# TensorE's order is written out by the program from the first mixer's projection on

## The chip, the cores and the metric

The kernel runs on one core of a Trainium2 chip. The time is the device time of one execution in microseconds (us): the median of three runs. PE is TensorE's matmul side, PEld its weight loads, DVE is VectorE, ACT ScalarE, POOL GpSimd, SP the engine that issues most of the DMAs. A code such as L466 is a line of the kernel.

## What is computed

Two decoder layers over 1024 tokens of width 1024. Only the first layer's mixer is touched by the change:

```python
h = rms_norm(x, norm_mix[l]) * (1.0 + scale_m) + shift_m   # scale_m, shift_m, ...: c_act @ w_ada + b_ada
# even_mixer:
proj = h @ w_in
u, q, k, v = jnp.split(proj, ...)
y = s5_ssm(u...);  y = gelu(y);  y = y * sigmoid(y @ w_glu)
q = apply_partial_rope(rms_norm(q, q_norm), cos, sin)       # k the same
o = diff_attention(q, k, v, lam, ...)                       # 4 heads, causal, 128-query blocks
mix = jnp.concatenate([y, o], axis=-1) @ w_out
x = x + gate_m * mix
x = x + gate_f * swiglu(...)                                # the first FFN; then the second layer
```

## The kernel before

A dense product in f32 accuracy is made of three matmuls for each slice of 128 inputs: the weights and the activations are each split into a rounded part and a rest (`whi`, `wlo` and the like), and `mm3g` (L466) adds hi x hi, lo x hi and hi x lo in PSUM. The weights are split by ACT (L449) and by DVE or POOL (L450).

The kernel is a set of Python generators. `weave(main, fill, rate)` advances `fill` by `rate` steps for each step of `main`, so the text of the program already interleaves the stages. What comes of it on an engine is decided by a scheduler: it runs a model of the engines and takes, for each engine, what it holds to be ready first. From the first FFN on (`manual_schedule` for PE, L1736) this is switched off for PE alone: there its instructions stand in the order in which the program issues them. DVE, ACT, POOL and SP are ordered by the scheduler throughout. Every engine works through its own list.

The stages that lie between the start and the first FFN, in the order of the program's text (`mix0`, L1147):

- `u_proj`: eight tiles `pu` of 24 matmuls, woven with `mods_acc`, which loads columns of `w_ada` (`mwt`), multiplies and adds them up on DVE into `macc` (L334, L336) and lets PE sum over the partitions (`mpc`, L391). Two such sums of 32 small matmuls are issued here, each after eight loads of 512 KB.
- `attn_proj(0)`, woven one to one with the four quarters of the state-space part (`s5_quarter`: `pS` L808, a scan on DVE L823, products on DVE and POOL L831 to L833, `pY` L840 and L842). `attn_proj(1)` follows, woven with the attention of heads 0 and 1 for the first 512 tokens.
- the attention of heads 2 and 3, woven with the gate's product `pz` (`glu`).
- the output projection `pout` (`out_proj(0)`), woven with 14 steps of the attention of the last 512 tokens.

`attn_proj(hp)` makes 24 tiles of 128 tokens by 256 columns: eight of q, eight of k, eight of v. A tile of q or k, in the order of the text, is this (L928 to L968):

```python
pt = pa.tile(...)                    # psA: two PSUM buffers
self.mm3(pt, ..., KT)                # 24 matmuls pq
nc.scalar.activation(sq, pt, AF.Square)                 # ACT  L945  asq
v.tensor_reduce(ss, sq, ...); v.tensor_scalar(ss, ...)  # DVE  L947, L948  ass
g_.tensor_tensor(rs, ss, mhalf, op=ALU.pow)             # POOL L950  ars
v.tensor_tensor(qn, pt, rs, op=ALU.mult)                # DVE  L952  aqn
g_.tensor_tensor(ra, ...); g_.tensor_tensor(rb, ...)    # POOL L959 to L962: rotary, into aqn
for h in range(2):
    nc.tensor.transpose(tp[:, h, :], qn[...], ident)    # PE   L965  tq
nc.scalar.activation(dst, tp, AF.Copy, scale=...)       # ACT  L967
yield
```

A tile of v has the 24 matmuls and one copy. An attention step has scores (`sps`, L1001 and a mask L1006), a maximum on DVE, exponentials on ACT, a combination on DVE, then transposes `wt` (L1039), a copy on ACT, the products with the values `po` (L1044), a norm over DVE, ACT and POOL, and the transpose `ot` (L1062).

Of the kernel before, what the change touches and what calls it, by code (L numbers as in the profile page):

```python
# [146 lines left out]
class Trunk:  # L147
# [1570 lines left out]
    def run(self):  # L1718
        st = self.stages
        nc, pool = self.nc, self.nc.gpsimd  # L1720
        self.setup()
        self.start()
        ffn0, ffn1, mix1 = "ffn0" in st, "ffn1" in st, "mix1" in st
        none = iter(())
        fs = {}
# [7 lines left out]
            drain(self.mods_acc(0, (2 * D, 6 * D), self.pz, "z", self.mods_tiles("C"), nc.sync))  # L1733
        if "mix0" not in st:
            self.late_vectors()
        ms = self.tc.manual_schedule(engines={mybir.EngineType.PE})  # L1736
        ms.__enter__()

        def mods1():
            if "mix0" in st:  # L1740
                self.close(self.ap)
                self.close(self.at)
                self.close(self.pss)
            self.close(self.pz)
            self.pr = self.open("m1p", 1, PSUM)
            if "mix0" in st:
                self.inject = self.glu_units(1)
            yield from self.mods_acc(1, (0, 6 * D), self.pr, "R", self.mods_tiles("C"), pool)
# [115 lines left out]
```

## Time and profile before

| | |
|---|---|
| median of 3 runs | 3177.56 us (3169.1 to 3178.48) |
| the profiled execution | 3189.24 us, span 3187.3 us |
| PE busy | 2976.2 us, 93% |
| DVE, ACT, POOL busy | 1921.7, 1193.9, 889.5 us |
| chain that ended last | PE 72%, DVE 12%, issue 6%, DMA 5% |
| mean granted TensorE clock | 0.965 |

The last matmul of `u_proj` starts at 143.6 us, the last of `attn_proj(1)` at 408.7, the sums that begin the first FFN's norm at 532.4, the first FFN's first matmul at 546.9. A busy PE isn't a PE at its peak: at the lower of its two clocks the same matmul is busy for longer. The granted clock is 1.00 at 2.4 GHz and 0.50 at 1.2 GHz.

### The profile page before, as it was taken

How to read it: one execution, taken by the hardware profiler on the slowest of the kernel's cores; microseconds unless marked ns; L12 is line 12 of the kernel's file. 1: busy time of each engine (PE TensorE's matmuls, PEld its weight loads, DVE VectorE, ACT ScalarE, POOL GpSimd, SP SyncE). 2: the span in 40 equal slices, each digit the busy share in tenths (PEclk: the TensorE clock that was granted, in tenths of full speed). 3: DMA queues.
4: the chain of work that ended last, by engine and by line, in shares of the span. 5: the costliest groups of instructions: out<-in, count | busy, mean ns of one | idle time of the engine just before them, and what ended most of it. 6: DMA issues, size and time to landing. Idle time of an engine off the chain costs nothing.

```text
span 3187.3 us, 50746 instructions
## 1 busy us (share of the span) xinstructions
PE 2976.2 (93%) x19326; PEld 2250.0 (71%) x19326; DVE 1921.7 (60%) x3982; ACT 1193.9 (37%) x2446; POOL 889.5 (28%) x1007
## 2 busy tenths in 40 slices
PE   4879989999999998999999999989999999999999
PEld 1678866776777766677666777666776677777777
DVE  7744645555674645777777545467777874434443
ACT  3212334333223644444444345544444443322222
POOL 6562402000110302344434342024344444200000
PEclk7989978999999999999999999999999999999999
DMA  6853221223573444212222244522222213533332
GB/s 242 213 134 67 69 71 53 80 73 105 179 232 113 156 146 126 71 56 77 74 67 80 81 148 136 155 85 75 70 60 81 75 59 93 167 90 93 96 103 93
DMA packets 489857, 338.39 MB, mean 106 GB/s; under 512 B 44280, under 2 KB 451088, under 8 KB 488592
## 3 DMA queue, kind: packets, MB, share of 16 engines
q1 hardware_dynamic: 474288, 304.75, 32.2%
q0 software_dynamic: 7632, 25.68, 2.6%
q10 hardware_dynamic: 7696, 4.74, 0.6%
q8 instruction: 153, 2.51, 0.3%
q14 instruction: 88, 0.72, 0.1%
HBM read 292.63 MB, written 42.47 MB: 105 GB/s over the span
## 4 chain that ended last, share of the span: by engine, by line
PE 72%; DVE 12%; issue 6%; DMA 5%; ACT 3%; POOL 2%; SPq 0%; ACTq 0%; DVEq 0%; POOLq 0%
PE pg L466 13%; PE pu L466 13%; PE pd L466 12%; PE pkrv L466 8%; PE pout L466 5%; PE pq L466 3%; PE sps L1001 3%; DMA mwt<-in_w_ada 2%; PE po L1044 1%; ACT whi L449 1%; PE pR L1666 1%; PE pA L1592 1%; PE pR L1651 1%; PE pA L1495 1%; DVE wlo L450 1%
## 5 line engine op out<-in xcount | busy, mean ns | idle before, releaser
L449 ACT CAST whi<-wraw 128x1024 fp32r<-128x1024 f32 (+2 forms) x472 | 401.9, 852 | 887.7 <-PE pg L466 186.3
L466 PE MATMUL pd<-dd,whi 128*128 128x512 f32 x1408 | 463.3, 410 | 14.8 <-DVE x L534 10.7
L450 DVE TENSOR_TENSOR wlo<-wraw,whi 128x1024 fp32r<-128x1024 f32 (+2 forms) x288 | 296.1, 1029 | 271.9 <-ACT whi L449 255.4
L450 POOL TENSOR_TENSOR wlo<-wraw,whi 128x1024 fp32r<-128x1024 f32 (+2 forms) x184 | 326.0, 1773 | 461.5 <-ACT whi L449 420.1
L466 PE MATMUL pg<-fhi,whi 128*128 128x512 f32 x704 | 301.5, 428 | 13.0 <-DVE sg L521 10.8
L466 PEld LDWEIGHTS pd<-dd,whi 128*128 128x128 f32 x1408 | 254.0, 189 | 80.6 <-ACT whi L449 19.3
L466 PE MATMUL pu<-fhi,whi 128*128 128x512 f32 x704 | 295.4, 420 | 1.4 <-ACT ev L1365 0.8
L466 PE MATMUL pg<-fhi,wlo 128*128 128x512 f32 x704 | 283.4, 403 | 6.3 <-DVE wlo L450 6.3
L466 PE MATMUL pu<-fhi,wlo 128*128 128x512 f32 x704 | 279.1, 396 | 3.7 <-POOL wlo L450 2.2
L466 PE MATMUL pg<-flo,whi 128*128 128x512 f32 x704 | 281.7, 400 | 0.0
L466 PE MATMUL pd<-dd,wlo 128*128 128x512 f32 x704 | 279.4, 397 | 2.1 <-DVE oss L1053 0.9
L466 PE MATMUL pu<-flo,whi 128*128 128x512 f32 x704 | 277.7, 394 | 0.0
L534 DVE SCALAR_TENSOR_TENSOR x<-pd,mod,x 128x512 f32<-128x512 f32 x192 | 143.4, 747 | 122.9 <-PE pd L466 121.9
L466 PE MATMUL pkrv<-xh,whi 128*128 128x512 f32 x384 | 165.4, 431 | 12.3 <-ACT ev L1365 6.4
L466 PEld LDWEIGHTS pg<-fhi,whi 128*128 128x128 f32 x704 | 135.2, 192 | 47.2 <-DVE sg L521 12.0
L466 PEld LDWEIGHTS pg<-fhi,wlo 128*128 128x128 f32 x704 | 135.1, 192 | 40.3 <-DVE wlo L450 8.7
L466 PEld LDWEIGHTS pd<-dd,wlo 128*128 128x128 f32 x704 | 133.0, 189 | 38.8 <-DVE wlo L450 3.8
L466 PEld LDWEIGHTS pu<-fhi,whi 128*128 128x128 f32 x704 | 132.9, 189 | 36.3 <-issue 2.4
L466 PEld LDWEIGHTS pu<-fhi,wlo 128*128 128x128 f32 x704 | 132.6, 188 | 35.7 <-POOL wlo L450 3.0
L466 PE MATMUL pkrv<-xh,wlo 128*128 128x512 f32 x384 | 154.6, 403 | 1.3 <-DVE wlo L450 1.3
L466 PE MATMUL pkrv<-xl,whi 128*128 128x512 f32 x384 | 154.4, 402 | 0.0
L466 PEld LDWEIGHTS pg<-flo,whi 128*128 128x128 f32 x704 | 135.3, 192 | 25.3
(460 smaller groups left out, 6084.1 us busy)
## 6 DMA issues: line engine op xcount, KB each, us to landing
wraw<-in_ffn_w_gate SPq DMA_DIRECT2D x88, 512.0 KB, 3.7
wraw<-in_ffn_w_up SPq DMA_DIRECT2D x88, 512.0 KB, 3.8
wraw<-in_ffn_w_down SPq DMA_DIRECT2D x128, 256.0 KB, 2.7
mwt<-in_w_ada POOLq DMA_DIRECT2D x48, 512.0 KB, 5.4
mwt<-in_w_ada SPq DMA_DIRECT2D x32, 512.0 KB, 5.4
wraw<-in_ffn_w_down SPq DMA_DIRECT2D x64, 192.0 KB, 2.5
kd<-ev SPq DMA_DIRECT2D x48, 256.0 KB, 2.0
xs<-x SPq DMA_DIRECT2D x8, 1024.0 KB, 6.3
```

What stands on the lines that cost most here:

```text
L449: nc.scalar.copy(hi, raw)
L450: (eng or nc.vector).tensor_tensor(lo, raw, hi.bitcast(F32), op=ALU.subtract)
L466: nc.tensor.matmul(out, lhsT=w(k), rhs=x(k), start=first and i == 0, stop=last and i == n - 1)
L534: nc.vector.scalar_tensor_tensor(x[:, n, :], pd, gate[:, n : n + 1], x[:, n, :], op0=ALU.mult, op1=ALU.add)
L1001: nc.tensor.matmul(sp[:, c0 : c0 + n], lhsT=qT[r : r + 64, hd, o : o + P], rhs=kT[r : r + 64, hd % 2, c0 : c0 + n], start=True, stop=not l ...
L1044: nc.tensor.matmul(po, lhsT=wt[:, j - j0, :], rhs=vt[:, j, P * (hd % 2) : P * (hd % 2) + P], start=(j == 0), stop=(j == i))
L1495: nc.tensor.matmul(pas[h][:, c, :], lhsT=FS[rows[h], c, :], rhs=AR[h][rows[h], c, :], start=True, stop=True)
L1592: te.matmul(px[32 * g : 32 * g + 32], lhsT=XF[:, g, :], rhs=QE[:, g], start=True, stop=True)
L1651: te.matmul(pp[rows[h], :], lhsT=AR[h][:, c, 0:64], rhs=XH[h][:, c, :], start=True, stop=True)
L1666: te.matmul(ph[rows[h], :], lhsT=BE[:, c, rows[h]], rhs=XU[h][:, c, :], start=True, stop=True)
```

## The change

The two lines that switch the scheduler off for PE are moved from behind the first mixer to ahead of it. `start()` stays scheduled; from `mix0()` on PE's instructions stand in the order of the text. No instruction is added or removed.

```diff
@@ run @@
         self.setup()
         self.start()
+
+        ms = self.tc.manual_schedule(engines={mybir.EngineType.PE})
+        ms.__enter__()
         ffn0, ffn1, mix1 = "ffn0" in st, "ffn1" in st, "mix1" in st
...
         if "mix0" not in st:
             self.late_vectors()
-        ms = self.tc.manual_schedule(engines={mybir.EngineType.PE})
-        ms.__enter__()
-
         def mods1():
```

The first place is PE at the start of `attn_proj(0)`. `pq_` and a number is one tile's PSUM buffer, `tq` its transposes, `mpc` the second sum of `mods_acc`. Before, the first tile's last matmul, the ends of the third and fourth tile, and what follows them:

```order
L466 MATMUL pq_1521<-whi_1517,m0lo_107_537 128x256
...
L466 MATMUL pq_1651<-whi_1517,m0lo_107_537 128x256
...
L466 MATMUL pq_1705<-whi_1517,m0lo_107_537 128x256
L965 MATMUL tq_1561<-ident,aqn_1553 128x128 x2
L391 MATMUL mpc_1456<-ones,macc_1139 32x1 x32
L808 MATMUL pS_1628<-UT_1565,s5E_13_157 64x128 x8
```

And now, from the end of `u_proj` on:

```order
L466 MATMUL pu_1426<-m0hi_169_1016,wlo_1357 128x512
L391 MATMUL mpc_1458<-ones,macc_1141 32x1 x32
L250 MATMUL vp_1501<-ident,vr_1492 128x104
L466 MATMUL pq_1523<-whi_1513,m0hi_104_534 128x256
...
L466 MATMUL pq_1523<-whi_1519,m0lo_107_537 128x256
L965 MATMUL tq_1563<-ident,aqn_1555 128x128 x2
L466 MATMUL pq_1586<-whi_1513,m0hi_104_534 128x256
...
L466 MATMUL pq_1586<-whi_1519,m0lo_107_537 128x256
L965 MATMUL tq_1626<-ident,aqn_1618 128x128 x2
L808 MATMUL pS_1630<-UT_1567,s5E_13_157 64x128 x8
```

The first tile's transposes stood behind four tiles; now every tile's transposes stand right behind its own 24 matmuls and ahead of the next tile's, and the same holds for all 32 tiles of q and k. The second sum `mpc` stood behind four tiles too, and now stands ahead of the first.

The second place is PE where `attn_proj(1)` has ended and `pz` begins. Before, behind the last `pq`:

```order
L1044 MATMUL po_4374<-vt_2852,wts_4377 128x128
L1001 MATMUL sps_4515<-kT_2851,qT_1505 128x512
...
L1001 MATMUL sps_4530<-kT_2851,qT_1505 128x512
...
L466 MATMUL pz_4348<-gluh_4328,whi_4344 128x512
L466 MATMUL pz_4348<-gluh_4329,whi_4344 128x512
L466 MATMUL pz_4348<-gluh_4328,wlo_4345 128x512
L466 MATMUL pz_4348<-gluh_4328,whi_4344 128x512
```

And now:

```order
L1001 MATMUL sps_4318<-kT_2853,qT_1507 128x128
...
L466 MATMUL pz_4350<-gluh_4330,whi_4346 128x512
L466 MATMUL pz_4350<-gluh_4331,whi_4346 128x512
L466 MATMUL pz_4350<-gluh_4330,wlo_4347 128x512
L1001 MATMUL sps_4354<-kT_2853,qT_1507 128x128
...
L1039 MATMUL wt_4377<-ident,pe_2844 128x128
L1001 MATMUL sps_4381<-kT_2853,qT_1507 128x256
```

Before, head 2 was done by then (the scores are those of its last block) and `pz` stood in two runs of 24 matmuls; now head 2 only begins here (a score over 128 keys is its first block), and `pz` is dealt out in threes and sixes over the steps of heads 2 and 3. Behind it `pout` follows in one run in the text's order, where before 36 of its matmuls stood between the steps of head 3. From the first FFN on PE's order is the same in both.

## Rows read from the trace of the kernel before

**Rows 1.** Busy time by stretch; columns: stretch, length, engines, granted clock, DMA, GB/s.

```profile
144.00:179.00 35.00, 19.34 (x165) 18.39 (x165) 17.99 (x22) 3.30 (x7) 29.41 (x29) 0.75 0.84 224
179.00:305.00 126.00, 114.51 (x846) 100.77 (x847) 57.07 (x126) 28.04 (x56) 46.49 (x81) 0.92 0.43 84
305.00:409.00 104.00, 100.69 (x860) 89.20 (x858) 63.03 (x190) 42.80 (x120) 42.15 (x88) 0.98 0.25 72
409.00:533.00 124.00, 115.56 (x460) 76.89 (x459) 60.59 (x137) 45.67 (x107) 19.37 (x17) 0.81 0.23 69
```

**Rows 2.** Instruction groups, 144 to 410 us: busy us, mean ns, idle before, releaser.

```profile
L466 PE MATMUL pq<-whi,m0hi 128*128 128x256 f32 x384 | 116.7, 305 | 16.4 <-DVE aqn L952 16.4
L842 PE MATMUL pY<-H,s5D 64*128 64x128 f32 x128 | 22.0, 316 | 5.6 <-DVE H L833 5.6
L1001 PE MATMUL sps<-kT,qT 64*128 64x128 f32 (+3 forms) x46 | 18.2, 475 | 0.0
L840 PE MATMUL pY<-UT 128*128 128x128 f32 x64 | 14.3, 313 | 0.0
...
L965 PE MATMUL tq<-ident,aqn 128*128 128x128 f32 x64 | 12.3, 279 | 0.0
...
L808 PE MATMUL pS<-UT,s5E 128*64 128x128 f32 x128 | 10.7, 299 | 0.0
L823 DVE TENSOR_TENSOR_SCAN s5tm<-rho,s5tm 128x128 f32<-128x128 f32 x32 | 10.6, 400 | 0.0
...
L1044 PE MATMUL po<-vt,wts 128*128 128x128 f32 x42 | 6.5, 279 | 0.0
...
L1039 PE MATMUL wt<-ident,pe 128*128 128x128 f32 x21 | 3.9, 272 | 0.0
```

**Rows 3.** Timeline, two tiles' norm and rotary: start us, duration us, engine, line, operation.

```profile
189.14 0.28 PE L466 MATMUL pq<-whi,m0lo 128*128 128x256 f32 x1
189.47 0.38 ACT L945 ACTIVATE asq<-pq 128x256 f32<-128x256 f32 x1
...
193.16 0.32 POOL L962 TENSOR_TENSOR aqn<-ara,arb 128x64 f32<-128x64 f32 x1
...
206.71 0.38 ACT L945 ACTIVATE asq<-pq 128x256 f32<-128x256 f32 x1 [9.18 <-PE pq L466]
...
211.03 0.32 POOL L962 TENSOR_TENSOR aqn<-ara,arb 128x64 f32<-128x64 f32 x1
```

**Rows 4.** Timeline of PE within one tile, behind a wait.

```profile
201.84 0.55 PE L466 MATMUL pq<-whi,m0hi 128*128 128x256 f32 x1 [5.37 <-DVE aqn L952]
202.19 0.41 PE L466 MATMUL pq<-wlo,m0hi 128*128 128x256 f32 x1
202.40 0.41 PE L466 MATMUL pq<-whi,m0lo 128*128 128x256 f32 x1
...
205.81 0.28 PE L466 MATMUL pq<-whi,m0hi 128*128 128x256 f32 x1
205.93 0.28 PE L466 MATMUL pq<-wlo,m0hi 128*128 128x256 f32 x1
```

**Rows 5.** Timeline of DVE: the second eight loads of `w_ada`, first, fourth, fifth, last.

```profile
145.09 1.14 DVE L334 TENSOR_SCALAR macc<-mwt,cact 128x1024 f32<-128x1024 f32 x1 [2.00 <-DMA mwt<-in_w_ada]
...
157.64 1.28 DVE L336 SCALAR_TENSOR_TENSOR macc<-mwt,cact,macc 128x1024 f32<-128x1024 f32 x1 [2.42 <-DMA mwt<-in_w_ada]
...
166.50 2.88 DVE L336 SCALAR_TENSOR_TENSOR macc<-mwt,cact,macc 128x1024 f32<-128x1024 f32 x1
...
176.79 1.28 DVE L336 SCALAR_TENSOR_TENSOR macc<-mwt,cact,macc 128x1024 f32<-128x1024 f32 x1 [2.15 <-DMA mwt<-in_w_ada]
```

**Rows 6.** The late attention steps: a 10 us stretch, then two transposes that begin a step.

```profile
450.00:460.00 10.00, 9.37 (x21) 4.82 (x21) 4.24 (x14) 3.48 (x13) 0.55 (x1) 0.50 0.00 1
...
449.44 0.42 PE L1039 MATMUL wt<-ident,pe 128*128 128x128 f32 x1
457.92 0.63 PE L1039 MATMUL wt<-ident,pe 128*128 128x128 f32 x2
```

## The prediction

> **What bounds the kernel now.** I read the page's busy shares first, then the chain that ended last, then busy time by stretch, then the groups and the timeline of the stretch that the change reaches. PE is busy for 93% of the span and holds 72% of the chain, so what PE loses ahead of the first FFN is paid at the end: from there on its order is the same in both, and nothing later has slack that would take a delay up. The stretch to read is 144 to 533 us, from the first `pq` to the first FFN's norm. Here PE is busy for 19.3 of 35, 114.5 of 126, 100.7 of 104 and 115.6 of 124 us [rows 1]: ragged at the start, then nearly closed, with 0.75, 0.92, 0.98 and 0.81 as the granted clock.
>
> It is closed because the scheduler puts matmuls behind something else whenever an operand isn't ready. The 64 transposes `tq` never once keep PE idle (their idle time is 0.0), while `pq` waits 16.4 us for a PSUM buffer to be read out by `aqn` [rows 2]. That zero is what the change touches: the order shows up to four tiles of `pq` between a tile and its `tq` before, and none now.
>
> **Step 1, the transposes of q and k.** What lies between a tile's last matmul and its `tq` is a chain over ACT, DVE, POOL, DVE and POOL. In a quiet place the last matmul begins at 189.14 and ends at 189.42, the square begins at 189.47, and the last rotary instruction ends at 193.16 + 0.32 = 193.48 [rows 3]: 4.06 us, and with a hand-off of 0.1 us (estimated from the gap of 0.05 at the chain's other end) 4.15 us. In a busier place the square begins at 206.71 and the chain ends at 211.35 [rows 3]: 4.64, with both ends 4.8 us. PE's list is worked off in order, so it stands for all of this, 32 times, with the next tile's 24 matmuls behind. I take 4.8, since DVE serves the state-space scan, the weight splits and the attention too; the bounds are 4.15 and 6.1, the latter with half of one quarter's scan (10.6 us / 8 = 1.3) [rows 2] in front.
>
> The Trainium skill says (TensorE: Matmul & The Clock Gate, "Step-by-step: what each phase is for") that only weight loads are pulled ahead and matmuls stay in program order. No run here shows a matmul that was free to pass a waiting one. By that rule the wait counts in full; without it, step 1 would be near zero and the kernel near 3178 us, which is the last rival below.
>
> **Step 2, the clock of the bursts between these waits.** After an idle time of 5.37 us a tile's matmuls follow each other at 0.21 us (202.19 to 202.40), and only from 205.81 at 0.12 [rows 4]: the lower clock for some 3.8 us, then the higher one. Before the stall the clock had not been low for good: the whole stretch averages 0.92 [rows 1]. A tile costs 24 x 0.117 = 2.8 us at the higher clock and 24 x 0.213 = 5.1 at the lower one. With a wait of nearly 5 us ahead of each, I take 3.8 us at the lower clock (18 matmuls) and the other 6 at the higher (0.7): 4.5 us. With 0.3 for the two transposes a tile of q or k takes 4.5 + 4.8 + 0.3 = 9.6 us, and 32 of them 307. Bounds: 2.8 + 4.15 + 0.3 = 7.25, so 232; 5.1 + 6.1 + 0.4 = 11.6, so 371.
>
> A rule of the skill bears on that (same page, "HAM oscillation — how this bites in real kernels"): bursts shorter than the waits between them start at half rate every time. By it the 32 bursts lose 32 x (4.5 - 2.8) = 54 us, and without it nothing; the rows above agree for one burst.
>
> **Step 3, the second `mpc`.** It needs eight loads of `w_ada`, added up on DVE at 145.09, ..., 157.64, 166.50, ..., 176.79 [rows 5]. Before, four tiles ran meanwhile; now the first `pq` is behind it. The fifth add was late (8.9 us after the fourth) since DVE was busy with the tiles' own work, which now comes later; the other six intervals average (31.7 - 8.9) / 6 = 3.8 us. So the sum is ready at about 145.1 + 7 x 3.8 + 1.3 = 173 us, and PE is idle from 144: 29 us. Bounds: 25 (intervals of 3.2) and 34 (as before, 178).
>
> **Step 4, what else stands in the stretch of 265 us, from 144 to 409 [rows 1].** The 16 tiles of v have no `tq` and run on: 16 x 2.8 + 3 for two slow starts = 48 (45 to 60). The state-space matmuls are 22.0 + 14.3 + 10.7 = 47 busy us [rows 2], some of it overlap of pipelined matmuls: 43 (35 to 60). They come behind a `tq`, not ahead of it, so they hide no wait. Attention now has 8 steps here where 11 ran; 11 took 18.2 + 6.5 + 3.9 = 28.6 us [rows 2], so 8 take 21 (16 to 32). Each quarter's scan, 10.6 / 4 = 2.7 us on DVE [rows 2], is queued ahead of one tile's chain: 12 (0 to 25). Sum: 29 + 307 + 48 + 43 + 21 + 12 = 460 us, against 265: +195. The ends all low: 353, or +88; all high: 582, or +317.
>
> **Step 5, heads 2 and 3, `pz` and `pout`.** Before, the scheduler had spent `pz` and a good part of `pout` early, so the last steps stood bare: at clock 0.50, one every 8.5 us [rows 6]. Now heads 2 and 3 (8 steps and the run-out) stand here with `pz` among them, and block 1's first steps fall among dense `pout`. 8 steps at about 8 us (less than 8.5, being shorter), 6 for the run-out, 192 `pout` of 512 columns at twice 0.117 = 45, and 12 for the other attention work: 127 against 124 [rows 1]. I take +3 (-15, if the filler keeps the clock up, to +20).
>
> Nothing else moves: the DMAs keep their order but for a few, and from the FFN on all is only later. So +198 on the profiled execution's 3189.24 us, or 3387; that execution stands 11.7 us above the median shown, so I forecast 3177.6 + 198 = 3376 us.
>
> **The rivals.**
> - The clock holds and the chains stay quiet: tiles at 7.25 us, the other terms low or as taken: 232 + 27 + 46 + 38 + 18 + 4 = 365, +100, 3278 us. For it: in 305 to 409 the clock was 0.98 [rows 1]; against it, that PE had no gaps there.
> - The chains are crowded: PE now waits for DVE, ACT and POOL, and in the second half attention's exponentials, maxima and copies queue among the chains (DVE 63.0, ACT 42.8 of 104 us [rows 1]). At 11.6 us a tile: 371 + 32 + 55 + 50 + 26 + 20 = 554, +289, 3467 us. Against it: none of these engines is over 61% busy.
> - Faster: the bare stretch of step 5 goes. From 440 to 488 us PE runs at half clock on attention alone; if `pz` and `pout`, now dealt out, keep it at the higher one, about half of it comes back, 25 us: 3153 us. It decides only if a tile's wait costs under 25 / 32 = 0.8 us; the shortest chain in the rows is 4.06.
> - It does nothing: PE passes the waiting transposes, or waits where it waited anyway. 3178 us. Against it: the order, and that PE already idles on `aqn` with other work in its list.
>
> **How the numbers follow.** The forecast 0.77, the holding clock 0.10, the crowded chains 0.10, faster 0.02, nothing 0.01. The forecast's own range is 3300 to 3440; taking in the first two rivals to their middle, 3280 to 3460. Faster than before by over 0.3% (what a measurement of this kernel can tell from none) 0.02, within it 0.01, slower 0.97.
>
> **What would show it.** Right: PE idle of 4 to 6 us ahead of `tq`, 32 times, put down to POOL's L962, some 150 us in sum; a granted clock well under 0.9 from 173 to the last `pq`; one wait near 29 us ahead of the second `mpc`; the last `pq` near 604 us; from the first FFN on the same lengths as before. Wrong: idle ahead of `tq` near 0, or of 3 us and less; a first `pq` ahead of 165 us; or a clock near 1.00 with tiles at 7 us.

## The result and the profile after

The kernel with TensorE's order given by the program from the projection on takes 3450.9 us (median of 4; 3445.1 to 3455.1) against 3174.1 for the kernel before (median of 4; 3169.1 to 3178.5): 1.0858 times as long, 95% interval 1.0830 to 1.0885, or 277 us more. The forecast was 3376 us, with 3300 to 3440 as its own range and 3280 to 3460 with its first two rivals taken in. The profiled execution took 3451.7 us (span 3449.9, mean clock 0.928), 262.5 more than that of before.

The time is lost ahead of the first FFN, as forecast. These are the busy times by stretch of the changed kernel, columns as in [rows 1]; up to 656 us stands what stood up to 409 before, then heads 2 and 3 and the output projection:

```profile
144.00:177.40 33.40, 10.53 (x153) 8.40 (x153) 23.42 (x12) 1.53 (x2) 18.72 (x9) 0.60 0.98 280
177.40:435.20 257.80, 178.64 (x930) 158.86 (x930) 59.12 (x127) 27.68 (x54) 48.82 (x91) 0.68 0.20 38
435.20:656.00 220.80, 145.85 (x853) 122.42 (x853) 64.83 (x176) 45.69 (x117) 39.20 (x88) 0.72 0.12 34
...
656.00:790.00 134.00, 114.99 (x478) 76.67 (x477) 67.36 (x161) 50.85 (x120) 16.91 (x17) 0.85 0.21 64
```

The first three are 512 us where [rows 1] shows 265, the last 134 where 124 stood. PE was idle for 30.5 of the 265 (265 less 234.5 busy) and is idle for 177 of the 512, and it is busy for 100.5 us more on nearly the same work, at a granted clock of 0.60 to 0.72 where it had 0.75 to 0.98. So there are two losses, idle time and a low clock.

From the FFN on hardly anything differs. This is the group of its first matmuls (count, ns min/median/max, first and last start), in the kernel before and in the changed one:

```profile
L466 PE MATMUL pg<-fhi,whi x704: 387/393/797, 547.0 to 3146.3; 128*128 128x512 f32 x176
```

```profile
L466 PE MATMUL pg<-fhi,whi x704: 387/394/797, 804.0 to 3408.2; 128*128 128x512 f32 x176
```

The first start is 257.0 us later, the last 261.9. The 5 us between have no place that I found. The kernels below, with the same order there, spread over 2632 to 2646 us from that first start to the end, so up to 14 us of a difference between two traces can lie there and not in what was changed.

The groups of 140 to 660 us that answer to [rows 2] (busy, mean ns, idle before):

```profile
L466 PE MATMUL pq<-whi,m0hi 128*128 128x256 f32 x384 | 138.7, 361 | 0.0
...
L842 PE MATMUL pY<-H,s5D 64*128 64x128 f32 x128 | 38.2, 448 | 1.2 <-DVE H L833 1.2
L1001 PE MATMUL sps<-kT,qT 64*128 64x128 f32 (+3 forms) x37 | 24.1, 749 | 0.0
...
L965 PE MATMUL tq<-ident,aqn 128*128 128x128 f32 x64 | 20.5, 420 | 148.9 <-POOL aqn L962 148.9
```

The zero ahead of `tq` has become 148.9 us, and the matmuls of every group shown are longer: `pY` 448 ns for 316, `sps` 749 for 475.

One tile of q shows both losses. The timeline of the changed kernel, answering to [rows 3] and [rows 4]:

```profile
456.83 0.42 PE L466 MATMUL pq<-wlo,m0hi 128*128 128x256 f32 x1
457.05 0.41 PE L466 MATMUL pq<-whi,m0lo 128*128 128x256 f32 x1
...
460.21 0.28 PE L466 MATMUL pq<-whi,m0lo 128*128 128x256 f32 x1
460.33 0.28 PE L466 MATMUL pq<-whi,m0hi 128*128 128x256 f32 x1
...
460.91 0.28 PE L466 MATMUL pq<-whi,m0lo 128*128 128x256 f32 x1
461.29 0.38 ACT L945 ACTIVATE asq<-pq 128x256 f32<-128x256 f32 x1 [3.27 <-PE pq L466]
...
464.79 0.32 POOL L962 TENSOR_TENSOR aqn<-ara,arb 128x64 f32<-128x64 f32 x1
465.16 0.69 PE L965 MATMUL tq<-ident,aqn 128*128 128x128 f32 x2 [3.96 <-POOL aqn L962]
```

The tile starts at the lower level, one matmul each 0.21 us, and only its last matmuls follow each other at 0.12. Then PE stands for 3.96 us, until the tile's own chain from the square to the last rotary instruction is done, and the clock is low again afterwards.

### The profile page after: what moved, and what is told of

It is laid out like the page before. It is cut to its first block, busy times and chain, and to the rows that moved or that the text cites. A ratio compares the mean times of both kernels' runs of the same rounds, so it can differ in the third digit from the quotient of the medians.

```text
span 3449.9 us, 50768 instructions
## 1 busy us (share of the span) xinstructions
PE 3069.2 (89%) x19326; PEld 2326.5 (67%) x19326; DVE 1942.1 (56%) x3982; ACT 1200.4 (35%) x2446; POOL 883.8 (26%) x1007
## 4 chain that ended last, share of the span: by engine, by line
PE 73%; DVE 13%; DMA 4%; ACT 4%; issue 3%; POOL 3%; SPq 0%; ACTq 0%; DVEq 0%; POOLq 0%
PE pg L466 13%; PE pu L466 13%; PE pd L466 11%; PE pkrv L466 7%; PE pq L466 5%; PE pout L466 4%; PE sps L1001 2%; DMA mwt<-in_w_ada 2%; ACT whi L449 1%; DVE wlo L450 1%; PE pY L842 1%; PE po L1044 1%; POOL ars L950 1%; PE pR L1666 1%; DVE macc L336 1%
```

## The experiments

Three theories were set against each other. Theory 1: the 32 waits of `tq` and the low clock around them are the loss. Theory 2: any order given by the program makes PE wait here, on one chain or another. Theory 3: the clock would be low in any case. Times are medians; each has the kernel before run beside it on the same chip (3171 to 3176 us).

### The transposes one tile later

```
@@ attn_proj
-                tp = self.ps.tile([P, 2, P], F32, tag="mm", name=self.nm("tq"))
...
+                late.append((qn, dst, n))
@@ behind the next tile's mm3
+                if len(late) >= 1:
+                    turn(*late.pop(0))   # the two transposes and the copy
```

> The changed kernel, with one thing moved in the program's text: the two transposes (tq) of a q or k tile, and the copy behind them, stand after the matmuls of the next tile instead of straight behind their own tile's norm and rotary chain. Theory 1 (the loss is the 32 waits of tq behind their own chain, 148.9 us in the changed kernel's trace, and the low clock that comes with these gaps, some 99.5 us more PE busy time in the stretch up to the last pq): nearly all of both comes back, the waits of tq fall below 30 us, the stretch runs near the 0.9 clock, and the time is 3215 to 3270 us; the wait of the second mpc (some 30 us) and some 10 us in heads 2 and 3 stay. Theory 2 (any order given by the program makes PE wait here, because the state-space and attention steps stand between the tiles with chains of their own): the waits move from tq to pY, wt and sps, over 100 us of idle stays, and the time is 3350 us or more.

3248.6 us (3245.2 to 3251.3), 1.0236 [1.0221, 1.0252] of the kernel before: 202 us of the 277 are back, as theory 1 had it. Its stretch from 144 us to the last `pq`, and the waits from 140 to 560 us, which takes in part of heads 2 and 3 (sum, times, longest):

```profile
144.00:468.00 324.00, 257.51 (x1937) 227.89 (x1938) 142.53 (x315) 73.23 (x172) 110.05 (x188) 0.83 0.32 82
```

```profile
PE mpc L391 <- DVE macc L336: 33.9, 2, 20.9
PE tq L930 <- POOL aqn L972: 27.2, 11, 6.6
PE wt L1046 <- DVE pe L1040: 12.2, 9, 3.0
```

Only the place of the 64 transposes, and of the copies behind them, differs from the changed kernel. Their wait fell from 148.9 to 27.2 us, and PE's busy time in the stretch from 335 to 257.5 us on the same matmuls: the clock came back with the gaps gone. The state-space and attention steps took little over: of the 12.2 us of `wt` only 3.9 lie in the stretch, where the changed kernel has 1.5, far from theory 2's 100.

### The gaps filled with matmuls that compute nothing

```
                 tp = self.ps.tile([P, 2, P], F32, tag="mm", name=self.nm("tq"))
+                for i in range(14):
+                    nc.tensor.matmul(tp[:, i % 2, :], lhsT=self.ident, rhs=self.ident, start=True, stop=True)
```

> The changed kernel with 14 matmuls of 128 columns that compute nothing of use (identity by identity into the tile that the transposes then overwrite) ahead of each tq, so that PE is at work for some 3.7 us (14 x 0.26) of the 3.9 us in which it now waits; the order and every wait on data stay. Theory 1: the wait as such costs 148.9 us and is now filled instead of idle, so that part stays; but PE has no gap, the clock rises to 2.4 GHz in the tiles, and the 99.5 us that the slower matmuls cost come back for the most part: 3345 to 3395 us, with granted clock above 0.85 from 180 us on. Theory 3 (the low clock is not due to these gaps): clock stays near 0.68, the fillers run at 1.2 GHz, take 14 x 0.42 = 5.9 us where 3.9 was idle, and the time goes up by some 64 us to about 3515.

3364.4 us (3357.2 to 3372.4): 86.5 us faster than the changed kernel, with 896 matmuls more. The stretch, and the fillers and true transposes in it:

```profile
144.00:573.50 429.50, 352.03 (x2833) 320.50 (x2834) 145.46 (x314) 75.16 (x172) 104.45 (x188) 0.86 0.26 61
```

```profile
L965 PE MATMUL tq<-ident 128*128 128x128 f32 x896 | 105.8, 276 | 0.0
L842 PE MATMUL pY<-H,s5D 64*128 64x128 f32 x128 | 23.0, 298 | 1.1 <-DVE H L833 1.1
...
L967 PE MATMUL tq<-ident,aqn 128*128 128x128 f32 x64 | 15.0, 320 | 50.3 <-POOL aqn L962 50.3
```

Fillers and remaining wait are 105.8 + 50.3 = 156 us where 148.9 were idle: the waits as such stay. The granted clock rose from 0.69 to 0.86, and the other matmuls are busy for 352.0 - 105.8 = 246 us where it was 335. (In this one execution the profile gives the higher level as 0.95 and not as 1.00: 0.95 from 2440 to 2980 us, without a fall to the lower level. A tile of v, with no gap ahead of it, takes 2.83 us there as in the changed kernel, so 0.86 understates the rise if anything.) This parts the two losses: some 150 us are the waits, some 85 the clock. Theory 3 is out.

### Without the rotary instructions

```
-                g_.tensor_tensor(ra, qn[:, :, 0:16], bc(C, 0, 16), op=ALU.mult)
-                g_.tensor_tensor(rb[:, :, 0:8], qn[:, :, 8:16], bc(Sn, 0, 8), op=ALU.mult)
-                g_.tensor_tensor(rb[:, :, 8:16], qn[:, :, 0:8], bc(Sn, 8, 16), op=ALU.mult)
-                g_.tensor_tensor(qn[:, :, 0:16], ra, rb, op=ALU.add)
```

> The changed kernel without the rotary part: the four GpSimd instructions that turn the first 16 columns of aqn, some 1.25 us of the 3.9 us between a tile's last matmul and its tq, are left out, so the rotation is missing from q and k. Theory 1 (each wait is the length of the tile's own chain): the 32 waits fall from 148.9 to some 110 us, put down to VectorE's aqn instead of GpSimd's, and the time by 39 us to about 3412, or to 3395 where the shorter gap also gives clock back. Rival (tq's start is set by something else, such as the copy or the tile buffers): waits and time stay, 3440 us or more.

3396.1 us (3386.0 to 3399.2), 54.8 less than the changed kernel. The waits on `tq`:

```profile
PE tq L955 <- DVE aqn L952: 111.1, 32, 9.2
```

37.8 us less in 32 waits, 1.18 each, where 1.25 of the chain was taken out: the wait is the chain's length. Up to the last `pq` the trace is 46 us shorter, so 8 more came from faster matmuls: PE is busy for 323.6 us where it was 334.6, at a clock of 0.71 for 0.69. The rest isn't the gaps' doing: from the first FFN matmul on this trace is 14 us shorter, with the same order there.

### The program's order from a later point

Both kernels enter the program's order inside `mix0`, one ahead of `attn_proj(1)`, one ahead of the steps of heads 2 and 3.

```
+        self.ms = self.tc.manual_schedule(engines={mybir.EngineType.PE})
+        self.ms.__enter__()
         drain(weave(self.attn_proj(1, at, self.pa, hh, hl), ...
```

> The program's order begins with the second half of the projection; pu, the modulation sums and the first half are placed by the scheduler as before. Theory 1 (the loss is so much per tile and adds up): in the changed kernel the first half ended 131.7 us later than before and the second half took 115 us more, so 3451 - 132 = 3319 us here (3300 to 3335), with 16 waits of tq of some 4 to 5 us each. Rival (the second half was slow because of the state it was left in, with a low clock and late sums): clearly less is lost, 3280 us or less.

3315.9 us (3310.6 to 3321.1), 135.0 less than the changed kernel where 131.7 were expected, with 16 waits of `tq` and 70.9 us (the second half of the changed kernel has 71.1). In the traces 123 us of it lie ahead of the last `pq` and 8 behind the first FFN matmul. The loss adds up by tiles, and the second half did not inherit it from the first.

> The program's order begins only behind the second half of the projection, with the steps of heads 2 and 3; everything before it is as the scheduler had it. Theory 1: the loss lies in the projection, and here only the last part's 11 us are lost: 3174 + 11 = 3185 us (3178 to 3195). Rival: the last part, the output projection and what follows carry a real share of the loss that the clock hides in the comparison of stretches: 3200 us or more.

3191.1 us, 1.0055 [1.0038, 1.0072]: slower by half a per cent, inside theory 1's range. The last stretch, and the waits that are new or longer in it (`ot` had 4.4 us before, `wt` none):

```profile
405.40:537.50 132.10, 111.65 (x474) 74.76 (x472) 66.37 (x158) 50.16 (x118) 16.91 (x17) 0.87 0.21 65
```

```profile
PE wt L1039 <- DVE pe L1033: 8.9, 6, 2.6
PE ot L1062 <- DVE os L1056: 8.1, 4, 4.4
```

### The second `mpc`

The first of these kernels has the transposes one tile later and enters the program's order behind `mpc`, ahead of `s5h` and `attn_proj(0)`. The others move the second eight of the `w_ada` loads to the later sums, in the changed kernel, in the one with the transposes one tile later, and in the kernel before.

```
-        drain(weave(self.u_proj(at, hh, hl), self.mods_acc(0, (2 * D, 4 * D), ...
+        drain(weave(self.u_proj(at, hh, hl), self.mods_acc(0, (2 * D, 3 * D), ...
...
-        mods = self.mods_acc(0, (4 * D, 6 * D), self.pz, "z", tiles, nc.sync, TB)
+        mods = self.mods_acc(0, (3 * D, 6 * D), self.pz, "z", tiles, nc.sync, TB)
```

> As the kernel with the transposes one tile later, but the program's order begins behind the first projection (pu) and the modulation sums, so that the scheduler places both mpc as in the kernel before. Theory 1: the second mpc cost some 30 us in the changed kernel beside all the rest, so this one is 25 to 35 us below the kernel with late transposes alone: 3185 to 3240 us. Rival: mpc only waited because PE had nothing else to do than wait for the same chain; then the first tiles are late by the weights or by the state-space chain instead, and the two kernels differ by less than 10 us.

3252.9 us (3248.7 to 3254.8), nothing below the 3248.6 with late transposes alone. Theory 1 missed here and the rival held. The timeline says why (VectorE, GpSimd and the first `tq`):

```profile
156.88 1.28 DVE L336 SCALAR_TENSOR_TENSOR macc<-mwt,cact,macc 128x1024 f32<-128x1024 f32 x1 [1.83 <-DMA mwt<-in_w_ada]
...
158.33 1.04 POOL L960 TENSOR_TENSOR ars<-ass,mhalf 128x4 f32<-128x4 f32 x1 [4.69 <-DVE ass L958]
159.36 1.89 POOL L772 TENSOR_TENSOR s5w<-s5W,s5t 128x1024 f32<-128x1024 f32 x1
...
161.21 1.89 POOL L773 TENSOR_TENSOR s5w<-s5W,s5t 128x1024 f32<-128x1024 f32 x1
...
165.73 2.34 POOL L774 TENSOR_TENSOR s5W<-s5w 128x1024 f32<-128x1024 f32 x1
...
168.02 1.30 POOL L972 TENSOR_TENSOR aqn<-ara,arb 128x64 f32<-128x64 f32 x1
...
169.38 0.69 PE L930 MATMUL tq<-ident,aqn 128*128 128x128 f32 x2 [12.02 <-POOL aqn L972]
```

The first tile's chain meets two others. On VectorE its `ass` stands behind a sum whose load came late, and GpSimd waits 4.69 us for it. Then GpSimd's products for the state-space weights (L772 to L774, 6.1 us) stand among the tile's own steps. In the kernel with late transposes alone these products ran while PE did the last of `pu` and stood at `mpc`; here the last of them (L777) ends 13 us later, VectorE stands 10.95 us for the load of the finished weights, up to 188.07 us, and the `tq` behind that waits 13.4 us where it was 6.6. `mpc`'s idle fell from 33.9 to 10.2 us, and that of `tq` rose from 27.2 to 46.4: the first tiles are late by the sums and the state-space chain instead, as the rival had it.

> The changed kernel with only this: the second eight of the w_ada loads, sums and their mpc moved to the later modulation sums. It prices the second mpc's wait by itself where tq still waits. Theory 1: some 20 to 30 us less than 3451, so 3420 to 3431 us. Rival (the wait only stands where the first tiles' chains would stand anyway, as in the kernel whose order began behind mpc): less than 10 us, 3441 us or more.

3431.8 us (3429.2 to 3434.9): 19.1 less than the changed kernel, just under theory 1's 20 to 30. That is close to the second `mpc`'s 20.8 us, but the trace doesn't put it there alone: `mpc`'s idle fell from 33.4 to 15.5 us, that of `tq` rose from 148.9 to 157.0, and of the 16.8 us between the two traces 13 lie ahead of the last `pq` and 5 behind the first FFN matmul.

> As the kernel with the transposes one tile later, and in addition the second eight of the w_ada loads with their VectorE sums and their mpc go with the later modulation sums, beside the second half of the projection; only the first eight stand beside pu. Theory 1: mpc's 33.9 us of idle fall to some 13 (the first mpc stays) and, other than in the kernel whose order began behind mpc, no tq takes the wait over, because the sums that stood ahead of the first tiles' chains on VectorE are gone too: 25 to 40 us less than 3249, so 3209 to 3224 us. Rival: the loads and sums come back in the second half, where attention waits for VectorE already (wt 12 us, ot 11 us): less than 12 us gained, 3237 us or more.

3243.9 us (3242.7 to 3251.4), not to be told from 3248.6: theory 1's 25 to 40 us didn't come. `mpc`'s idle fell from 33.9 to 17.2 us, but `tq` waits 35.1 us where it was 27.2, and PE is busy for 263.1 us of the stretch where it was 257.5. I did not settle what makes the difference to the kernel just above, where `tq` took over some 8 us as well.

> The kernel before (scheduler's order) with the second eight of the w_ada loads, sums and their mpc moved to the later modulation sums. Theory 1: the scheduler had put the projection's first tiles into that wait, so that there is little to gain: within 12 us of 3174. Rival: VectorE's sums hold up the first tiles' chains there too (pq waited 16.4 us for aqn): 3150 to 3162 us.

3181.2 us, 1.0011 [0.9985, 1.0037]: no difference that can be measured, as theory 1 had it. The scheduler had hidden that wait.

### The transposes two tiles later, and combinations

```
-                if len(late) >= 1:
+                if len(late) >= (1 if n == "v" else 2):
                     turn(*late.pop(0))
```

> As the kernel with the transposes of a tile behind the next tile's matmuls, but two tiles later. There 27.2 us of waits of tq on their chains were left, the longest ones behind the state-space scan's block, and the granted clock of the stretch was 0.83. Theory 1 (each wait costs itself and the clock behind it): the 27.2 us fall below 12 and some of the 23 us of slower matmuls come back: 3215 to 3238 us. Rival: what is left of those waits is a queue on VectorE (scan, sums) that two tiles don't cover either, and the time stays within 8 us of 3249.

3232.3 us (3230.0 to 3239.6), 1.0171 [1.0134, 1.0209]: as theory 1 had it. No wait of `tq` is left in the list, and the clock up to the last `pq` is 0.89. The longest waits from 140 to 480 us:

```profile
PE mpc L391 <- DVE macc L336: 34.1, 2, 22.1
PE wt L1046 <- DVE pe L1040: 10.1, 8, 3.0
PE pS L808 <- DMA UT<-us: 10.0, 1, 10.0
PE pq L466 <- DVE aqn L962: 7.6, 3, 3.8
```

Two combinations, both with the transposes two tiles later, give the program's order to the two halves of the projection alone (and from the first FFN on, as before):

```
         self.late_vectors()
+        ms = self.tc.manual_schedule(engines={mybir.EngineType.PE})
+        ms.__enter__()
...
+        ms.__exit__(None, None, None)
         drain(weave(self.attn_steps(0, (2, 3), ap, self.pa), self.glu(0), 1))
```

> Scheduler's order up to the modulation sums; program order only for the two halves of the projection, with the transposes two tiles later and the second eight of the w_ada loads and sums moved to the later modulation sums; scheduler's order again for heads 2 and 3 and the output projection, and the program's order from the first FFN on, as before. Theory 1, by sum: 3232 us of the kernel with transposes two tiles later, less some 28 us of mpc waits, less 8 to 11 us of the last stretch, less up to 10 us of the wait for the state-space input: 3185 us, 3170 to 3200, still not below the kernel before at 3171. Rival (as the last runs showed, mpc's wait is only partly paid back): 3205 us or more.

> The same without moving the second eight of the w_ada loads. Theory 1: with two tiles between a tile and its tq, the first tiles run while VectorE still makes the sums, so the 25 us that the first tq waited in the kernel with one tile between shrink to 10 or less: 3195 us (3180 to 3210), 5 to 15 us above the kernel with the sums moved. Rival: the sums on VectorE hold the first chains and so the tile buffers however late tq stands: 15 us or more above it.

3231.2 us (3215.7 to 3235.3) and 3215.3 (3211.4 to 3224.9). Theory 1 missed both times: the first is 46 us above its sum, where its rival (3205 us or more) had put it, and the second, in which the sums stay early, is 16 us below the first and not above, against its rival too. In the first `mpc` waits only 4.0 us, but the waits went to the state-space steps, which the program's text puts between the tiles (in the second `mpc` waits 25.4 us and `pY` 1.6):

```profile
PE pY L840 <- DVE s5tm L816: 12.1, 1, 12.1
PE wt L1046 <- DVE pe L1040: 10.6, 3, 4.5
PE pS L808 <- DMA UT<-us: 10.1, 1, 10.1
PE pY L842 <- DVE H L833: 8.7, 3, 6.0
```

So what is left is of theory 2's kind: with the 32 waits gone, a fixed order still stands at `pY`, `pS`, `wt` and `mpc`, each once or a few times. The best of these kernels is 1.0118 [1.0089, 1.0146] of the kernel before; none beats it.

## Why the prediction was right, and where its sum was short

Slower was forecast at 0.97, at 3376 us; it came to 3451. The mechanism was the one named. The size was short: 198 us were forecast and 277 measured, outside the forecast's own 3300 to 3440. That it lies within 3280 to 3460 is in part luck, since that range was widened for the rival of the crowded chains, whose mechanism didn't come. Of the 75 us by which the forecast was short, 52 lie in the stretch below and 7 in step 5; 5 lie behind the first FFN matmul, and 11 come from the starting point, as the kernel before was profiled in an execution above its median and the changed one near its median.

The terms of the stretch from 144 us to the last `pq`, in us; "measured" goes by PE's timeline, from each row's start to the next one's, with the idle time of a row put to what waited:

| Term | Forecast | Measured |
|---|---|---|
| up to the first `pq` | 29 | 33.5 |
| 32 tiles of q and k | 32 x 9.6 = 307 | 32 x 9.71 = 311 |
| of each: matmuls, wait, transposes | 4.5 + 4.8 + 0.3 | 4.65 + 4.65 + 0.41 |
| 16 tiles of v | 48 | 51.5 |
| state-space matmuls | 43 | 70 |
| attention | 21 | 43 |
| scan ahead of a chain | 12 | in the waits |
| the late `mpc`, one weight split | 0 | 3 |
| sum (before: 265) | 460 | 512 |

**Step 1, right.** 32 waits, put down to POOL's L962, 148.9 us; forecast 32 x 4.8 = 154 and 12 for the scan. They are not spread as I had it: 25 of them are 3.89 to 3.96 us, the quiet chain and a little under my lower bound of 4.15, one is 4.21, and six are 5.1 to 11.2, where DVE, and in some POOL, served something else first (the scan and the products behind it, weight splits, sums). TensorE passed no waiting transpose; with the wait's length following the chain's in the kernel without rotary, this is shown.

**Step 2, right, by experiment too.** A tile's 24 matmuls took 4.65 us on average (4.5 forecast), and with the gaps filled 3.39; from row to row the projection's matmuls take 200.3 us in all with the gaps and 156.0 with them filled. Of the 32 tiles 27 begin at one matmul each 0.21 us, and five at 0.12. The Trainium skill's rule (TensorE: Matmul & The Clock Gate, "HAM oscillation — how this bites in real kernels") is that bursts shorter than the waits between them start at half rate every time. The trace agrees for those 27 tiles, though most bursts here are longer than the usual wait of 3.9 us.

**Step 3, the size nearly right.** The second sum was ready at 176.33 us (forecast 173), but PE did not stand idle for 29 us ahead of it. I had overlooked the first `mpc`: the program's order holds `pu`'s last tile behind it too, so that PE stood 12.6 us there, then did the 8.5 us of `pu` that I took as done by 144, and stood 20.8 us at the second:

```profile
146.04 1.03 PE L391 MATMUL mpc<-ones,macc 128*32 128x1 f32 x64 [12.57 <-DVE macc L336]
...
176.33 1.03 PE L391 MATMUL mpc<-ones,macc 128*32 128x1 f32 x64 [20.79 <-DVE macc L336]
```

I also misread why the fifth add was late in the kernel before: VectorE was not busy, it stood 5.12 us for a tile's square, with the add behind it. And I had not seen that passing this wait gains little where the first tiles' chains share VectorE with those sums, and GpSimd with the state-space weights.

**Step 4, mis-sized: the term that made the sum short.** I priced the state-space and attention matmuls from their groups in the kernel before, where the clock was 0.92 to 0.98, and kept the lower clock for the q and k bursts alone. But they stand between the same gaps: 70 us for 43 and 43 for 21, both above my upper bounds of 60 and 32, and together 49 of the 52 us by which the sum was short. The filled kernel shows what of it was the clock: `pY` took 57.7 us from row to row in the changed kernel and 33.8 with the gaps filled (31.7 in the kernel before), attention's four groups 39.5 and 27.8. So of attention's 22 us 12 are the clock and 3 are waits; the other 7 are a wrong count. I took 8/11 of all of it and left out the masks and `ot`, but only the scores became fewer (32 for 44): `po`, `wt` and `ot` ran 40, 20 and 8 times where they had run 42, 21 and 8. The rival of the crowded chains (11.6 us a tile, 3467 us) came nearer to the time than the forecast, but not by its mechanism: the tiles took 9.7.

**Step 5, the sign right.** 134 for 124, +10 where +3 was forecast. In the kernel that leaves all else to the scheduler the whole costs 17 us by the medians, and 9 in the traces, from the last `pq` to the first FFN matmul; `wt` and `ot` wait there for VectorE (8.9 and 10.7 us, against 4.4 for `ot` in the kernel before). That this is so because no `pout` stands between them any more goes by the order and was not tested. The stretch of [rows 6], at a clock of 0.50 there, has become one at 0.64 in which PE is busy for 20.5 of 33 us:

```profile
656.00:690.00 34.00, 28.19 (x104) 17.42 (x104) 20.23 (x59) 15.05 (x43) 1.67 (x3) 0.80 0.38 120
690.00:723.00 33.00, 20.46 (x60) 10.78 (x58) 15.20 (x50) 11.32 (x35) 2.69 (x5) 0.64 0.07 21
```

**What stays open.** With the transposes two tiles later 58 us are left. The second `mpc` (19 us by itself) and the last stretch (17) were priced in other kernels, and that they add up here was not shown: with the last stretch, and what stands ahead of the projection, given back to the scheduler 17 us came back, with the second `mpc` moved as well only 1. The rest lies in the waits listed there and was not taken apart.

## What to carry to other kernels

Before an engine's order is fixed, list each instruction that stands straight behind a chain over other engines: its price is the chain's length, times its count, plus the lower clock for all that runs between these gaps, the neighbours too. Move such an instruction one or two tiles later in the text: here that brought 202 and 219 of 277 us back. And taking one wait away pays only if no other chain (here sums on VectorE that wait for loads, and the state-space weights on GpSimd) holds the next instruction as well.

## What the runs showed that I had not expected

- 896 matmuls of no use made the kernel 86.5 us faster, as the granted clock of the stretch went from 0.69 to 0.86.
- A gap shorter by 1.18 us in 32 places made the trace up to the last `pq` 46 us shorter, 8 more than the gaps themselves.
- The late sums were worth 19.1 us in the changed kernel and nothing that can be measured in the scheduler's order or with the late transposes.
